# VectorE alone makes the low halves of all weight units: GpSimd's share of them is taken away

## The chip, the cores and the metric

The kernel runs on one core of a Trainium2 chip. The metric is the device time of one execution in microseconds (us), given as the median of several executions. TensorE (PE) multiplies matrices, ScalarE (ACT), VectorE (DVE) and GpSimd (POOL) do the elementwise work, and SyncE (SP) issues the weight transfers. In the profile PEld is TensorE's weight load.

## The reference

Two models of depth 2 run one after the other on 256 tokens of width 1024, in float32. What matters here is how many weights pass through:

```python
# first block, layer 0
x = layer_norm(ALPHA * x + retention_mixer(x, ret_w_in, ret_w_out))
x = layer_norm(ALPHA * x + swiglu(x, ffn_w_in, ffn_w_out))          # D_FF = 2816
# first block, layer 1
x = layer_norm(ALPHA * x + stick_breaking_mixer(x, k, v, w_q, w_out))
x = layer_norm(ALPHA * x + moe_swiglu(x, w_router, w_in, w_out))     # 8 experts, top 2, D_EXPERT = 3584
# second block, two layers
x = x + rms_norm(hybrid_mixer(rms_norm(x), w_in, ..., w_out))        # dilated attention and mLSTM
x = x + rms_norm(conv_ffn(rms_norm(x), w_up, ..., w_down))
```

Every product is a float32 one, and every weight is used once for all tokens that need it.

## The kernel before, in words

**Weight units.** All big weights are cut into 519 units of 128 partitions by 2048 columns (`UNIT`), 1 MB each, in the order of use. `Stream` (line 33) loads them ahead of use on SyncE's queue. A float32 product is made of three products of float32r parts: a unit is split into a high half `wh`, which ScalarE makes by a copy that rounds (`split_h`, line 75), and a low half `wl`, which is the unit minus its high half (`split_l`, line 89). TensorE then multiplies high by high, high by low and low by high. At most four units (three in the experts' phase) are split and not yet used up; `done()` after a unit's last product frees its place, and the next `advance()` splits the next unit.

**Who makes the low half.** `split_l` cuts the 2048 columns at `cut`: VectorE subtracts columns 0 to `cut`, GpSimd the rest, each in an instruction of its own. `W.cut` is set by hand from phase to phase, and `W.order`, if it isn't empty, gives the cuts of the next units one by one. With `cut` = UNIT VectorE makes the whole half, with 0 GpSimd does. In the first three phases (retention, ffn, stick-breaking) most units have `cut` = UNIT; in the experts' phase, the two conv_ffn phases and all their output projections it is 1408, in most of the two hybrid phases 1024.

**Joints.** Between two phases stands a joint: the last four units of the output projection are used by token tile (`tail`, line 252), so that the norm of the first 128 tokens (`joint.stats(0)`, then `joint.trans(0)`, which transposes its result and splits it) lies beside the products of the second 128. In the `advance()` calls between them the first four units of the next phase are split; their cuts are `Joint.order` = 0, UNIT, 0, 1024 (in stick-breaking 1024, 0, 0; after the experts 0, 0; at the experts' start UNIT, 0, then UNIT four times). `head` (line 273) then multiplies the first three units by the first token tile, runs `joint.trans(1)`, and multiplies the fourth.

**Order.** The program's order is the order of each engine's queue (there is no scheduler): a weight split stands in VectorE's queue where `advance()` was called, between the instructions of the norms, the gates and the attention. In the experts' phase a step is one slice of one expert: four units of its input weights and two of its output weights, 72 matmuls of 512 columns. Every second expert has a step in which `regather` (line 705) splits the 256 tokens again (line 648, two instructions on VectorE). In the last expert GpSimd also scales and adds the residual (lines 899 and 900). GpSimd's queue also issues the small transfers: gains, tables, convolution weights.

Of the kernel before, what the change touches and what calls it, by code (L numbers as in the profile page):

```python
# [10 lines left out]
F32 = mybir.dt.float32  # L11
# [5 lines left out]
OP = mybir.AluOpType  # L17
# [12 lines left out]
UNIT = 2048  # L30


class Stream:
    """Weights in units of [128, UNIT]: loaded, then split into two float32r parts, ahead of use."""

    def __init__(self, nc, pool, pairs, raws, units):
        self.nc, self.pool, self.units = nc, pool, units
        self.pairs = self.room = pairs
        self.free = [(pool, "raw%d" % i, len(units)) for i in range(raws)]
        self.order, self.cut = [], UNIT  # L40
        self.n_load = self.n_h = self.n_l = self.n_get = self.n_done = 0
        self.rt, self.ht = {}, {}

    def widen(self, slots):
        """More slots (pool, tag, end) for loads, each for units before its end."""
        self.free = slots + self.free

    def slot(self):
# [31 lines left out]
    def split_l(self):  # L80
        i = self.n_l
        if i >= self.n_h:
            return False
        (r, s), h = self.rt.pop(i), self.ht[i]
        l = self.part("wl")
        cut = self.order.pop(0) if self.order else self.cut
        for eng, s0, s1 in ((self.nc.vector, 0, cut), (self.nc.gpsimd, cut, UNIT)):
            if s0 < s1:
                eng.tensor_tensor(l[:, s0:s1], r[:, s0:s1], h[:, s0:s1].bitcast(F32), op=OP.subtract)  # L89
        self.ht[i] = (h, l)  # L90
        self.free.append(s)
        self.n_l += 1
        self.load()
        return True
# [34 lines left out]
class Net:  # L129
# [108 lines left out]
                                          start=(first and kk == 0 and i == 0), stop=(last and kk == 1 and i == 2))  # L238

    def proj_out(self, yh, yl, n, joint):  # L240
        """n units of the output projection, its last four by token tile, with the joint's parts between."""
        accs = [self.psA(), self.psA()]
        m = 4
        for u in range(n - m):
            w = self.W.get()
            for t in range(2):
                self.out_unit(accs[t], w, yh, yl, u, t, u == 0, False)
            self.W.done()
            self.W.advance()
        self.tail(accs, [(yh, yl, u) for u in range(n - m, n)], n == m, joint)  # L250

    def tail(self, accs, items, first, joint, hooks=()):
        m = len(items)
        ws = [self.W.get() for _ in range(m)]
        for i, (yh, yl, u) in enumerate(items):
            if i < len(hooks):
                hooks[i]()
            self.out_unit(accs[0], ws[i], yh, yl, u, 0, first and i == 0, i == m - 1)
        self.W.advance()
        joint.stats(0, accs[0])  # L260
        accs[1] = accs[1] or self.psA()
        for i, (yh, yl, u) in enumerate(items):
            self.out_unit(accs[1], ws[i], yh, yl, u, 1, first and i == 0, i == m - 1)
            self.W.done()
            if i == m - 2:
                joint.trans(0)
            if i in joint.early:
                self.W.advance()
        joint.stats(1, accs[1])
        if joint.order[-1] is not None:  # L270
            self.W.advance()

    def head(self, joint, table, n=4):
        """The first n units of the next projection by token tile, the second tile's joint between."""
        ws, ps = [], []
        for i in range(n):
            if i == n - 1:
                joint.trans(1)
                self.nc.scalar.preload_act_table_set(table + "_and_others")
            ws.append(self.get8())  # L280
            ps.append(self.psP([128, 2, 256]))
            self.tokB(ps[i], ws[i], 0)
        self.W.cut = UNIT
        for i in range(n):
            self.tokB(ps[i], ws[i], 1)
            self.W.done()
            yield ps[i]

    def features(self, first, n, pool):
        """The n feature-major products of a projection whose first units came by token tile."""  # L290
        nc, last = self.nc, None

        def copied(ps):
            x = pool.tile([128, 2, 256], F32, tag="fl", name="fl", bufs=2)
            nc.scalar.activation(x, ps, AF.Copy)
            return x

        def flip(x):
            pt = self.psP([128, 2, S])
            for c in range(2):  # L300
                for t in range(2):
                    nc.tensor.transpose(pt[:, c, tok(t)], x[:, t, tok(c)], self.ident)
            return pt

        k = 0
        for ps in first:
            x = copied(ps)
            if last is not None:
                yield flip(last)
            last = x  # L310
            k += 1
        ps = self.projA()
        yield flip(last)
        yield ps
        for _ in range(n - k - 1):
            yield self.projA()
# [145 lines left out]
    def stick(self, joint0):  # L462
# [107 lines left out]
        parts(7)  # L570
        joint = LayerNorm(self, o, w, 2, "kT")
        joint.early = (0, 1, 2)
        joint.order = [1024, 0, 0, None]

        def last():
            pv(6)
# [6 lines left out]
        return joint  # L583

    def open_moe(self):
        """Room for the experts' first weights, before the phase itself."""
        W = self.W
        self.mp = p = self.span.enter_context(self.tc.tile_pool(name="m1", bufs=1))
        self.moe_i = i = W.n_get
        end = i + 6 * E * SL  # L590
        W.widen([(p, "yy", i + 44)] + [(p, "more%d" % j, end) for j in range(2)])
        while W.load():
            pass

    def moe(self, joint0):
        nc, tc, a, W = self.nc, self.tc, self.a, self.W
        with self.span:
# [1 line left out]
            end = self.moe_i + 6 * E * SL  # L599
            W.widen([(self.xt, "x%d" % (self.x_tag ^ 1), self.moe_i + 46)])  # L600
            W.load()
            W.cut, W.order = 1408, [UNIT, 0] + [UNIT] * 4
            low, ones, slot = self.low[:, 0, :], self.low[:, 1, :], self.slot
            x = self.x
            X3 = {}
# [179 lines left out]
                return yh, yl  # L785

            def sums(n):
                """Both halves of an expert's output, in one or two tiles."""
                A = [self.psA() for _ in range(n)]
                if n == 1:  # L790
                    return [A[0][:, f, :] for f in range(2)], [(A[0].rearrange("p f c -> p (f c)"), slice(0, D))]
                return [x[:, 0, :] for x in A], [(A[f][:, 0, :], half(f)) for f in range(2)]
# [15 lines left out]
                        nc.vector.tensor_tensor(o, q, o, op=OP.add)  # L808

            def overflow():  # L810
                """Every expert's tokens beyond its first 128 (not run when there are none)."""
                most = nc.values_load(mci[0:1, 0:1], min_val=0, max_val=2 * S)
                ov_w, ov_x = (x.rearrange("p k s -> p (k s)") for x in self.new_xT())
                ov_h, ov_l = ov_w[:, :D], ov_w[:, D:]
# [112 lines left out]
                W.split_l()  # L927
            joint.trans(0)
            W.advance()
            W.cut = 1408  # L930
            combine(*part, 1, False)
            joint.stats(1, acc[:, 1, :])
            W.advance()
# [2 lines left out]
    def hybrid(self, l, joint0):  # L936
        nc, tc, a, W = self.nc, self.tc, self.a, self.W
        with tc.tile_pool(name="h1", bufs=1) as p, tc.tile_pool(name="h2", bufs=2) as w:
# [67 lines left out]
            dn = {}  # L1006

            def rotated(ps):
                """Queries or keys of four heads, token-major."""
                x = w.tile([128, 2, 4, 2, 32], F32, tag="cv", name="ro")  # L1010
                t1, t2 = (w.tile([128, 2, 8, 32], F32, tag="wk", name=n) for n in ("t1", "t2"))
                for t, i in ((t1, 0), (t2, 1)):
# [15 lines left out]
                    nc.scalar.activation(dst[0], ps, AF.Copy, scale=scale)  # L1028

            def attend(n):  # L1030
                """The turn of head n - 1's probabilities and the scores of head n."""
                A = self.psA()
                if n > 0:
                    x = at[:, (n - 1) % 2]
# [136 lines left out]
                nc.vector.reciprocal(rs, rs)  # L1171

            def gated(i, ps):
                """Output gates of heads 2i, 2i+1, doubled, by the gain."""
                c = slice(256 * i, 256 * i + 256)
                nc.scalar.activation(sg[:, :, c], ps, AF.Tanh, scale=0.5)
                nc.vector.scalar_tensor_tensor(sg[:, :, c], sg[:, :, c], 1.0,
                                               hg[:, None, c].to_broadcast([128, 2, 256]), op0=OP.add, op1=OP.mult)
# [5 lines left out]
                        nc.vector.scalar_tensor_tensor(y, y, rs[:, 2 * h + t:2 * h + t + 1], sg[:, t, tok(h)],  # L1184
                                                       op0=OP.mult, op1=OP.mult)

            W.cut = UNIT
            first = self.head(joint0, "natural_log_exp")
            aq = {}
            todo = {1: [(prepare,)], 3: [(gating,)], 5: [(gates, 0)], 6: [(gates, 1)], 7: [(mscores, 0), (mscores, 1)],  # L1190
# [2 lines left out]
            for u in range(14):  # L1193
# [3 lines left out]
                    i = u - 1  # L1197
                    flip([qk[:, i % 2, i // 2 * 2:i // 2 * 2 + 2]], aq.pop(i), 0, 1.0 if i % 2 else 0.125)
                c = None
                if u == 0:  # L1200
                    W.cut = 1408
                if u < 4:
                    aq[u] = rotated(ps)
                elif A:
# [25 lines left out]
                    f[0](*f[1:])  # L1230
                if u == 4:
                    nc.scalar.preload_act_table_set("exp_and_others")
                    W.cut = 1024
                if u not in (3, 13):
                    W.advance()
            mnorm()
# [11 lines left out]
    def conv_ffn(self, l, joint0):  # L1248
        nc, tc, a, W = self.nc, self.tc, self.a, self.W
        with tc.tile_pool(name="c1", bufs=1) as p, tc.tile_pool(name="c2", bufs=2) as w:  # L1250
# [4 lines left out]
            for j, ps in enumerate(self.features(self.head(joint0, "gelu_apprx_tanh"), FT, w)):  # L1255
# [4 lines left out]
                for c in range(2):  # L1260
# [2 lines left out]
                                                   op0=OP.mult, op1=OP.add)  # L1263
                    nc.vector.scalar_tensor_tensor(u[:, c, :S - 1], ps[:, c, 1:], k[:, 2:3], u[:, c, :S - 1],
                                                   op0=OP.mult, op1=OP.add)
                W.cut = 1408
                more = W.split_h()
                nc.scalar.activation(u[:, 0, :], u[:, 0, :], AF.Gelu_apprx_tanh)
                nc.vector.tensor_tensor(u[:, 0, :], u[:, 0, :], u[:, 1, :], op=OP.mult)
# [1 line left out]
                    W.split_l()  # L1271
                self.split(yh[:, j, :], yl[:, j, :], u[:, 0, :])
                W.advance()
            W.cut = 1408
            self.proj_out(yh, yl, FT // 2, joint)
            return joint


class Joint:
    early = (0, 2)  # L1280
    order = (0, UNIT, 0, 1024)

    def __init__(self, net, p, w):
        self.n, self.nc, self.p, self.w = net, net.nc, p, w
# [7 lines left out]
    def begin(self):  # L1292
        n = self.n
        self.xo = n.x
        self.xn = n.new_x()
        n.W.cut, n.W.order = 1024, [x for x in self.order if x is not None]
        self.nc.scalar.preload_act_table_set("sqrt_and_others")
        self.src = {}

# [61 lines left out]


class MoeNorm(LayerNorm, PreNorm):
    order = (0, 0)

    def __init__(self, net, p, w, i, pre):
        Joint.__init__(self, net, p, w)
        g = p.tile([128, 2, D], F32, tag="oh", name="jg")
# [196 lines left out]
```

## Time and profile before

| what | value |
|---|---|
| time, median of 3 | 2355.78 us (2352.26 to 2356.99) |
| span of the profiled execution | 2346.5 us |
| median less that span | 9.3 us |
| matmuls in the span | 13077 |
| TensorE's mean granted clock | 0.983 of full speed |
| weights and other bytes moved | 562.16 MB, 240 GB/s over the span |

The profiled execution's time outside its span is not listed by itself; its time is taken as the span and the 9.3 us that lie between it and the median, a difference that has the spread of the three executions (4.7 us) in it. The engines run side by side, so shares of busy time don't add up. A matmul's duration in the profile overlaps the next one's, so TensorE is at its peak only where its clock is 1.00 and its next matmul waits for nothing.

### The profile page before, as it was taken

How to read it: one execution, taken by the hardware profiler on the slowest of the kernel's cores; microseconds unless marked ns; L12 is line 12 of the kernel's file. 1: busy time of each engine (PE TensorE's matmuls, PEld its weight loads, DVE VectorE, ACT ScalarE, POOL GpSimd, SP SyncE). 2: the span in 40 equal slices, each digit the busy share in tenths (PEclk: the TensorE clock that was granted, in tenths of full speed). 3: DMA queues.
4: the chain of work that ended last, by engine and by line, in shares of the span. 5: the costliest groups of instructions: out<-in, count | busy, mean ns of one | idle time of the engine just before them, and what ended most of it. 6: DMA issues, size and time to landing. Idle time of an engine off the chain costs nothing. (4 is left out here: it accounts for less than half of the span.)

```text
span 2346.5 us, 33318 instructions
## 1 busy us (share of the span) xinstructions
PE 2235.6 (95%) x13077; PEld 1932.6 (82%) x13077; DVE 1739.7 (74%) x1655; ACT 1370.8 (58%) x1376; POOL 1282.4 (55%) x523
## 2 busy tenths in 40 slices
PE   8999999997999999999999999987998999999998
PEld 8997998886887788778877788766887997887996
DVE  6556554647899898988897889977775984775982
ACT  4353543564776677767776677765555654555662
POOL 4002000213899889889997889896333234434333
PEclk9999999998999999999999999998999999999999
DMA  8454554436989799979997899966334554433552
GB/s 311 144 174 155 203 188 161 171 133 260 361 321 338 258 382 353 353 286 368 350 351 289 317 372 359 352 250 225 111 111 161 198 198 162 146 108 137 198 198 72
DMA packets 80085, 562.16 MB, mean 240 GB/s; under 512 B 9072, under 2 KB 9136, under 8 KB 13488
## 3 DMA queue, kind: packets, MB, share of 16 engines
q1 hardware_dynamic: 76464, 547.39, 63.6%
q0 software_dynamic: 3456, 12.55, 1.5%
q8 instruction: 105, 1.72, 0.3%
q14 instruction: 60, 0.49, 0.1%
HBM read 558.86 MB, written 1.05 MB: 239 GB/s over the span
## 5 line engine op out<-in xcount | busy, mean ns | idle before, releaser
L89 POOL TENSOR_TENSOR wl<-raw,wh 128x640 fp32r<-128x640 f32 (+2 forms) x436 | 1200.7, 2775 | 845.8 <-ACT wh L75 749.1
L89 DVE TENSOR_TENSOR wl<-raw,wh 128x1408 fp32r<-128x1408 f32 (+2 forms) x503 | 1108.7, 2218 | 332.7 <-ACT wh L75 274.5
L75 ACT ACTIVATE wh<-raw 128x2048 fp32r<-128x2048 f32 x518 | 990.9, 1915 | 421.7 <-PE pp L750 146.1
L201 PE MATMUL pp<-xh,wh 128*128 128x256 f32 x1360 | 387.9, 285 | 7.3 <-ACT wh L195 7.3
L201 PE MATMUL pp<-xh,wl 128*128 128x256 f32 x1360 | 387.2, 285 | 0.9 <-DVE wl L89 0.9
L201 PE MATMUL pp<-xl,wh 128*128 128x256 f32 x1360 | 384.0, 282 | 0.0
L201 PEld LDWEIGHTS pp<-xh,wh 128*128 128x128 f32 x1360 | 257.7, 189 | 8.8 <-ACT wh L195 7.8
L201 PEld LDWEIGHTS pp<-xl,wh 128*128 128x128 f32 x1360 | 259.1, 191 | 0.2 <-issue 0.2
L201 PEld LDWEIGHTS pp<-xh,wl 128*128 128x128 f32 x1360 | 256.1, 188 | 2.1 <-DVE wl L89 1.1
L201 PE MATMUL pp<-wl,xh 128*128 128x256 f32 x720 | 205.1, 285 | 7.1 <-POOL wl L89 4.7
L201 PE MATMUL pp<-wh,xh 128*128 128x256 f32 x720 | 208.0, 289 | 2.1 <-DVE mix L1139 2.1
L201 PE MATMUL pp<-wh,xl 128*128 128x256 f32 x720 | 203.5, 283 | 0.0
L750 PE MATMUL pp<-wl,xh 128*128 128x512 f32 x448 | 180.2, 402 | 11.9 <-POOL wl L89 7.8
L750 PE MATMUL pp<-wl,xgh 128*128 128x512 f32 x448 | 179.6, 401 | 9.0 <-DVE wl L89 8.2
L750 PE MATMUL pp<-wh,xgh 128*128 128x512 f32 x448 | 181.1, 404 | 5.0 <-DVEq L827 5.0
L750 PE MATMUL pp<-wh,xh 128*128 128x512 f32 x448 | 180.8, 404 | 0.0
L750 PE MATMUL pp<-wh,xl 128*128 128x512 f32 x448 | 179.1, 400 | 0.0
L750 PE MATMUL pp<-wh,xgl 128*128 128x512 f32 x448 | 178.5, 398 | 0.0
L201 PEld LDWEIGHTS pp<-wl,xh 128*128 128x128 f32 x720 | 137.6, 191 | 11.2 <-POOL wl L89 6.8
L760 PE MATMUL pa<-wh,hh 128*128 128x512 f32 x448 | 142.2, 399 | 0.7 <-ACT hh L195 0.7
L760 PE MATMUL pa<-wl,hh 128*128 128x512 f32 x448 | 141.4, 397 | 0.0
L760 PE MATMUL pa<-wh,hl 128*128 128x512 f32 x448 | 141.4, 397 | 0.0
(338 smaller groups left out, 3343.6 us busy)
## 6 DMA issues: line engine op xcount, KB each, us to landing
raw<-in_moe_w_in SPq DMA_DIRECT2D x224, 1024.0 KB, 5.1
raw<-in_moe_w_out SPq DMA_DIRECT2D x112, 1024.0 KB, 5.2
raw<-in_w_up SPq DMA_DIRECT2D x44, 1024.0 KB, 4.8
raw<-in_w_in SPq DMA_DIRECT2D x28, 1024.0 KB, 5.0
raw<-in_ret_w_in SPq DMA_DIRECT2D x23, 1024.0 KB, 5.0
raw<-in_ffn_w_in SPq DMA_DIRECT2D x22, 1024.0 KB, 4.9
raw<-in_w_down SPq DMA_DIRECT2D x22, 1024.0 KB, 4.8
raw<-in_ffn_w_out SPq DMA_DIRECT2D x11, 1024.0 KB, 4.8
```

The costliest lines, as they stand in the source:

```text
L75: self.nc.scalar.activation(h, self.rt[i][0], AF.Copy)
L89: eng.tensor_tensor(l[:, s0:s1], r[:, s0:s1], h[:, s0:s1].bitcast(F32), op=OP.subtract)
L201: self.nc.tensor.matmul(out, lhsT=w, rhs=x, start=(i == 0), stop=(i == n - 1))
L750: nc.tensor.matmul(q, lhsT=x[:, k, :], rhs=ww[:, kk, :], start=(k == 0 and i == 0), stop=(k == KC - 1 and i == 2))
L760: nc.tensor.matmul(A[0][f], lhsT=x[:, k, :], rhs=ww[:, kk, half(f)], start=(s == 0 and k == 0 and i == 0), stop=(s == SL - 1 and k == 3 an ...
```

## The change

Every low half is now one VectorE instruction over all 2048 columns (the first unit, which `start` splits in quarters, was VectorE's before and stays so). `cut` and `order` are gone, with all the lines that set them; `joint.order[-1] is not None`, which also told whether the tail ends with an `advance()`, becomes `joint.after`, with the same values. The order of loads, of high halves and of all other work in the queues is as before, and comments in the code were taken out.

```diff
@@ class Stream, split_l
         (r, s), h = self.rt.pop(i), self.ht[i]
         l = self.part("wl")
-        cut = self.order.pop(0) if self.order else self.cut
-        for eng, s0, s1 in ((self.nc.vector, 0, cut), (self.nc.gpsimd, cut, UNIT)):
-            if s0 < s1:
-                eng.tensor_tensor(l[:, s0:s1], r[:, s0:s1], h[:, s0:s1].bitcast(F32), op=OP.subtract)
+        self.nc.vector.tensor_tensor(l, r, h.bitcast(F32), op=OP.subtract)
         self.ht[i] = (h, l)
...
@@ tail
-        if joint.order[-1] is not None:
+        if joint.after:
             self.W.advance()
@@ stick
-        joint.order = [1024, 0, 0, None]
+        joint.after = False
@@ moe
-            W.cut, W.order = 1408, [UNIT, 0] + [UNIT] * 4
@@ hybrid (other places that set W.cut likewise)
-                    W.cut = 1024
@@ class Joint
     early = (0, 2)
-    order = (0, UNIT, 0, 1024)
+    after = True
@@ Joint.begin
-        n.W.cut, n.W.order = 1024, [x for x in self.order if x is not None]
@@ class MoeNorm
-    order = (0, 0)
-
```

## Rows read from the trace of the kernel before

**Rows 1.** The page: busy time of each engine, share of the span, instructions.
```profile
PE 2235.6 (95%) x13077; PEld 1932.6 (82%) x13077; DVE 1739.7 (74%) x1655; ACT 1370.8 (58%) x1376; POOL 1282.4 (55%) x523
```

**Rows 2.** TensorE's waits by releaser: us in total, times, longest.
```profile
PE pp L750 <- DVE wl L89: 12.3, 3, 4.3
PE pp L750 <- POOL wl L89: 8.5, 5, 4.3
```

**Rows 3.** Stretches of the experts' phase: busy us of the engines, granted clock, DMA.
```profile
600.00:1560.00 960.00, 937.45 (x4153) 754.90 (x4152) 836.12 (x469) 669.75 (x459) 874.55 (x316) 0.99 0.89 334
780.00:800.00 20.00, 15.73 (x72) 12.67 (x71) 15.40 (x10) 10.16 (x9) 13.93 (x6) 0.91 0.79 278
1040.00:1060.00 20.00, 15.90 (x69) 12.84 (x68) 14.57 (x9) 9.60 (x8) 13.10 (x6) 0.83 0.78 281
1300.00:1320.00 20.00, 16.04 (x70) 12.83 (x69) 16.03 (x11) 10.55 (x8) 13.17 (x6) 0.91 0.81 291
```

**Rows 4.** Groups by shape, whole span: count, busy us, mean ns, idle before.
```profile
L89 DVE TENSOR_TENSOR wl<-raw,wh 128x1408 fp32r<-128x1408 f32 x395 | 877.6, 2239 | 186.4 <-ACT wh L75 128.5 <-POOL wl L89 46.3 <-PE pp L750 5.6
L89 DVE TENSOR_TENSOR wl<-raw,wh 128x2048 fp32r<-128x2048 f32 x82 | 190.2, 2323 | 113.0 <-ACT wh L75 112.9
L89 DVE TENSOR_TENSOR wl<-raw,wh 128x1024 fp32r<-128x1024 f32 x26 | 40.9, 1571 | 33.3 <-ACT wh L75 33.1
L196 DVE TENSOR_TENSOR hl<-pp,hh 128x512 fp32r<-128x512 f32 x56 | 38.0, 679 | 2.1 <-ACT hh L195 2.1
...
L89 POOL TENSOR_TENSOR wl<-raw,wh 128x640 fp32r<-128x640 f32 x395 | 1044.8, 2668 | 331.7 <-ACT wh L75 235.0 <-DVE u L1262 77.5 <-DVE wl L89 6.9
L89 POOL TENSOR_TENSOR wl<-raw,wh 128x2048 fp32r<-128x2048 f32 x15 | 73.8, 4928 | 346.3 <-ACT wh L75 346.3
```

**Rows 5.** Timeline, one unit of an output projection: start, duration, instruction, idle before.
```profile
1955.75 1.63 DVE L89 TENSOR_TENSOR wl<-raw,wh 128x1408 fp32r<-128x1408 f32 x1 [4.01 <-ACT wh L75]
1955.79 3.01 POOL L89 TENSOR_TENSOR wl<-raw,wh 128x640 fp32r<-128x640 f32 x1 [2.63 <-ACT wh L75]
```

**Rows 6.** Groups by shape in one experts' step, 653.79 to 671.29 us.
```profile
L89 DVE TENSOR_TENSOR wl<-raw,wh 128x1408 fp32r<-128x1408 f32 x6 | 16.3, 2747 | 0.1
...
L89 POOL TENSOR_TENSOR wl<-raw,wh 128x640 fp32r<-128x640 f32 x7 | 20.4, 2954 | 0.0
```

**Rows 7.** Timeline at the first `regather`: VectorE, TensorE.
```profile
778.60 4.51 DVE L648 TENSOR_TENSOR x3ol<-x,x3oh 128x1024 fp32r<-128x1024 f32 x2
...
786.04 0.51 PE L750 MATMUL pp<-wl,xgh 128*128 128x512 f32 x1 [4.27 <-DVE wl L89]
```

**Rows 8.** Timeline of the last joint but one; and a line of the chain.
```profile
2140.86 2.76 DVE L89 TENSOR_TENSOR wl<-raw,wh 128x2048 fp32r<-128x2048 f32 x1 [1.01 <-ACT wh L75]
2142.70 5.38 POOL L89 TENSOR_TENSOR wl<-raw,wh 128x2048 fp32r<-128x2048 f32 x1 [1.23 <-ACT wh L75]
2145.04 3.59 DVE L1405 TENSOR_TENSOR x<-z,x 128x512 f32<-128x512 f32 x1
2153.14 1.22 DVE L89 TENSOR_TENSOR wl<-raw,wh 128x1024 fp32r<-128x1024 f32 x1 [0.19 <-ACT wh L75]
2156.67 0.39 PE L201 MATMUL pp<-wl,xh 128*128 128x256 f32 x1 [0.58 <-POOL wl L89]
...
1822.52 97.91 PE pp L201 x816
```

**Rows 9.** Timeline of a unit in the first hybrid phase.
```profile
1727.14 1.23 DVE L89 TENSOR_TENSOR wl<-raw,wh 128x1024 fp32r<-128x1024 f32 x1 [2.27 <-ACT wh L75]
1727.18 3.45 POOL L89 TENSOR_TENSOR wl<-raw,wh 128x1024 fp32r<-128x1024 f32 x1 [9.53 <-ACT wh L75]
1729.34 1.31 DVE L1054 TENSOR_SCALAR nm<-m 128x2 f32<-128x2 f32 x1
```

**Rows 10.** Timeline, TensorE in the first joint.
```profile
216.65 0.75 PE L1308 MATMUL pp<-ident,x 128*128 128x128 f32 x3 [1.96 <-DVE x L1329]
```

**Rows 11.** Timeline, TensorE at the start of the first conv_ffn.
```profile
1815.67 0.66 PE L302 MATMUL pp<-ident,fl 128*128 128x128 f32 x4 [3.30 <-ACT fl L295]
```

More of the change, by code (lines that the diff above doesn't have):

```diff
@@ L39, in __init__ @@
         self.free = [(pool, "raw%d" % i, len(units)) for i in range(raws)]
-        self.order, self.cut = [], UNIT
         self.n_load = self.n_h = self.n_l = self.n_get = self.n_done = 0
@@ L282, in head @@
             self.tokB(ps[i], ws[i], 0)
-        self.W.cut = UNIT
         for i in range(n):
@@ L929, in moe @@
             W.advance()
-            W.cut = 1408
             combine(*part, 1, False)
@@ L1185, in mfinal @@
                                                        op0=OP.mult, op1=OP.mult)
-            W.cut = UNIT
             first = self.head(joint0, "natural_log_exp")
@@ L1199, in hybrid @@
                 c = None
-                if u == 0:
-                    W.cut = 1408
                 if u < 4:
@@ L1265, in conv_ffn @@
                                                    op0=OP.mult, op1=OP.add)
-                W.cut = 1408
                 more = W.split_h()
@@ L1273, in conv_ffn @@
                 W.advance()
-            W.cut = 1408
             self.proj_out(yh, yl, FT // 2, joint)
```

## The prediction, as it was put on record

> **What bounds the kernel now.** I read the page first: TensorE is busy 95% of the span, so no more than the rest, and what a lowered clock costs, is to be had; VectorE has 74%, GpSimd 55% [rows 1]. Next come TensorE's waits. The two that name low halves in the experts' phase are 12.3 us in three waits on VectorE's part and 8.5 us in five on GpSimd's [rows 2]. The table of stretches shows what such a wait costs beside itself: in the 20 us that begin with each of the three, TensorE's granted clock averages 0.91, 0.83 and 0.91 where 1.00 is full speed (2.4 GHz), so part of each ran at the lower level of 1.2 GHz after the idle time; (0.09 + 0.17 + 0.09) x 20 us = 7.0 us [rows 3]. In the 960 us from 600 to 1560 TensorE is idle 22.5 us in all. Outside the waits the experts' phase is bound by TensorE, and no change in the splitting makes that faster.
>
> **What the subtraction costs on the two engines.** The groups by shape hold the main clue: 1408 columns take VectorE 2239 ns, 2048 columns 2323 ns [rows 4]. The short instruction is as long as the long one, because most short ones ran beside GpSimd and most long ones did not. The timeline shows how: both parts start together, VectorE's ends after 1.63 us, GpSimd's after 3.01 us [rows 5]. If GpSimd's 640 columns begin only when VectorE is through, they take 3.01 - 1.63 = 1.4 us. So the two take turns, and a unit costs the pair about 3.0 us one after the other where VectorE alone needs 2.3. The turns go the other way too: a GpSimd unit of 5.38 us from 2142.70 ends at 2148.08, and a VectorE addition begun at 2145.04 ends 0.55 us after that, having taken 3.59 us [rows 8]; in the hybrid phase an instruction over two columns takes 1.31 us and ends at 1730.65, as GpSimd's part does (1727.18 + 3.45) [rows 9].
>
> **The change part by part.**
>
> *Work moved.* VectorE gets 395 x (2.32 - 2.24) = 32 us for the units cut at 1408, 26 x (2.32 - 1.57) = 20 us for those at 1024, and 15 x 2.32 = 35 us for GpSimd's whole ones: 87 us, against holds that end in its other instructions. GpSimd loses at least 1045 + 74 of its 1282 us [rows 1, 4]. Its instructions of line 89 and their waits go; no transfer is added, and raw buffers come free no later.
>
> *Experts, `regather`.* In a plain step of 17.5 us VectorE's six parts take 2747 ns each with no idle time and GpSimd's seven 2954 ns [rows 6]: the pair is as full as TensorE and has no slack. `regather`'s two instructions (4.51 us with the turns) then delay everything, and TensorE waits 4.27 us [rows 7]; the three waits are of this kind [rows 2]. After the change a step holds 6 x 2.32 + 2 x 0.68 = 15.3 us of VectorE work [rows 4], 2.2 us less than the step. `regather` itself should fall to an estimated 2.4 us (two times 1.22, what 1024 columns take alone [rows 8]). ScalarE's copies before it still delay the next high half, so I leave an estimated 1.2 us of each wait, and count no lowered clock behind it (a choice; the lower bound holds the other case). Gain: 12.3 + 7.0 - 3 x 1.2 = 15.7 us; bounds 6 (half of the wait left and the clock still falling) and 19.3.
>
> *Experts, the last one.* Five waits of 8.5 us [rows 2] come where GpSimd's residual work stands in its queue ahead of its parts. With no part there, the wait goes; GpSimd's residual instructions stay and still take turns with VectorE. Taken: 7; bounds 3 and 10.
>
> *Joints.* The third unit moves from GpSimd into VectorE's queue ahead of the norm of the second tile. In the joint of [rows 8] VectorE's second unit ends at 2140.86 + 2.32 = 2143.2 and its third at 2145.5; the norm's scaling comes next, an estimated 1.0 us before the addition, which then starts at 2146.5 unheld and ends an estimated 1.2 us later at most (its 512 columns are half of a 1.22 us instruction), against 2148.63. I take the chain as 1.5 us earlier. The fourth unit then begins at 2151.6 and takes 2.32 instead of 1.22 us, ready at 2154.0. Before, TensorE had half of that unit's product behind it when GpSimd's half arrived at 2156.67; half a product is 12 x 97.91/816 = 1.4 us, so it stood where it would have started at 2155.2. Gain 1.2 us each, three such joints: 3.7. The two LayerNorm joints after retention and ffn also lose the wait of 1.96 us [rows 10] but pay the same 1.1 us on the fourth unit: 2.5 each, 5. Stick-breaking's, where three units now stand ahead of VectorE's norm: 1.3. The joint after the experts, where two units move ahead of its second norm: 0. Sum 10; bounds -3 (each of seven loses 0.4) and 16.
>
> *Start of conv_ffn.* The small transfers stand behind GpSimd's part of the fourth unit; they go earlier, and VectorE's first product there is no longer held. TensorE's wait is 3.30 us [rows 11]; the second conv_ffn has a shorter one. Taken 4 for both, bounds 0 and 5.
>
> *Hybrid.* Here VectorE's chain sets the pace at places. Its part goes from 1.23 to 2.32 us, 1.1 later; but the short instruction behind it, now held until 1730.65, would end at 1727.14 + 2.32 and then what stood between 1728.37 and 1729.34 (0.97) and an estimated 0.2: 1730.63 [rows 9]. So the ten units of a phase change nothing; the starts of the phases, where the turns hold the rotary products, give an estimated 1 us each, the gating at the end 0.5. Taken 3, bounds -21 (20 units of 1.09 us, were all on TensorE's path) and 6.
>
> On splitting, the measured side is that a part of 1024 columns is ready after 1.22 us and a whole unit after 2.32, and TensorE could begin on the part [rows 4, 8]. The Trainium skill (Perfetto Trace Analysis, Optimizing Scalar/DVE Operations) says that where VectorE isn't saturated but leaves bubbles on other engines, breaking instructions up may finish work sooner, and that a saturated VectorE may hand work to GpSimd, though the port they share may spoil that. The first half speaks against one long instruction; it is the second rival's mechanism, and the row of 3.01 us for two parts is why I give it little.
>
> **Sum.** 15.7 + 7 + 10 + 4 + 3 = 39.7 us off the profiled execution: 2346.5 - 39.7 = 2306.8 of span, and with the 9.3 us between span and median 2316.
>
> **The rivals.** *VectorE becomes the bound among the experts.* Combining and gathering add to the 15.3 us of some steps and bring them to TensorE's 17.5; then the waits move rather than go, and the experts give only their lower bounds, 6 + 3: 2330. For it: VectorE is already busy 836 of 960 us [rows 3]. Against: much of that is time held. *VectorE's queue, the slower outcome.* A unit of 2.32 us in one piece stands in front of the short chains: 20 hybrid units at 1.09 and 15 moved whole units at 2.32 are 21 + 35 = 56 us; less the experts' 22.7 and conv_ffn's 4, the kernel is 29 us slower: 2385. It decides where the held time that goes is under half of the added time; in [rows 9] it is all of it. *The turns aren't what stretches the parts*, and the change does only half of what it says: TensorE's phase is full anyway, the joints win and lose, and the time stays within 0.2% (2351 to 2360). *More than forecast:* with fewer waits the clock stays at its upper level in the joints and hybrids too, and the upper bounds hold (19.3 + 10 + 16 + 5 + 6 = 56): 2299.
>
> **How the numbers follow.** Forecast near 2316 (2306 to 2326): 0.52. VectorE bound among the experts (2326 to 2345): 0.20. More than forecast (2290 to 2306): 0.17. No change: 0.05. Slower: 0.06. The range 2295 to 2342 leaves out the last two and the outer ends of the second and third. A difference under 0.2%, 4.7 us, which is also the spread of the three executions, can't be told from none: faster 0.90, same 0.04, slower 0.06.
>
> **What would show it.** In the changed kernel's groups all 395 + 82 + 26 + 15 = 518 low halves of line 89 on VectorE in one shape at 2.25 to 2.35 us, none on GpSimd; TensorE's waits on low halves under 6 us in the experts' phase and clock 1.00 after `regather`; line 648 near 1.2 us each; the addition of [rows 8] under 1 us. I am wrong if whole units take over 2.6 us beside the transfers, if the hybrid phases grow by more than 5 us each, or if the three waits are still over 3 us.

## The result, and the profile after

The changed kernel takes 2300.39 us (median of 4 executions, 2299.26 to 2307.82) against 2356.03 us (2352.26 to 2356.99), a ratio of 0.9774 with a 95% interval of 0.9756 to 0.9792: 55.6 us faster. The forecast was 2316 (2295 to 2342). The profiled execution took 2301.24 us with a span of 2299.5 us, 47.0 less than the span of before; the forecast for the span was 39.7 less.

The page's line of busy times, which answers to [rows 1]: GpSimd goes from 55% to 4%, and VectorE, which now does the work of both, from 1739.7 to 1711.3 us.

```profile
PE 2220.5 (97%) x13077; PEld 1929.2 (84%) x13077; DVE 1711.3 (74%) x1670; ACT 1373.2 (60%) x1376; POOL 88.1 (4%) x87
```

The groups by shape of the changed kernel, whole span, as [rows 4]: all 518 low halves have one shape and 2300 ns each.

```profile
L85 DVE TENSOR_TENSOR wl<-raw,wh 128x2048 fp32r<-128x2048 f32 x518 | 1187.8, 2300 | 312.7 <-ACT wh L74 295.1 <-PE pp L744 7.5 <-DVEq L821 2.3
```

VectorE's low halves take 1187.8 us in place of 877.6 + 190.2 + 40.9 = 1108.7 [rows 4], 79 more, and yet it is busy 28 us less: its other instructions, the same in number, lost 107.5 us, which was time held. Its low halves of before had held time in them too, which `pieces` below measures: 395 x (2239 - 1628) ns = 241 us. The same experts' step as in [rows 6], by shape: six whole units take 13.7 us where six short parts took 16.3.

```profile
L85 DVE TENSOR_TENSOR wl<-raw,wh 128x2048 fp32r<-128x2048 f32 x6 | 13.7, 2291 | 2.0 <-ACT wh L74 2.0
```

TensorE's waits after (us in total, times, longest; the first is the low halves waited for in the joints, the second answers to [rows 2]), and the stretch from 600 to 1560 us with the 20 us around each `regather` (columns as in [rows 3]): the waits fell from 20.8 to 2.0 us, and the clock stays at 2.4 GHz, 1.00, where it averaged 0.91, 0.83 and 0.91.

```profile
PE pp L197 <- DVE wl L85: 8.9, 6, 1.6
...
PE pp L744 <- DVE wl L85: 2.0, 3, 0.9
```

```profile
600.00:1560.00 960.00, 954.31 (x4266) 773.01 (x4265) 838.36 (x481) 688.60 (x472) 23.70 (x11) 1.00 0.91 345
770.00:790.00 20.00, 19.48 (x94) 15.83 (x93) 17.36 (x11) 15.38 (x13) 0.00 (x0) 1.00 0.89 324
1020.00:1040.00 20.00, 19.49 (x94) 15.80 (x93) 18.67 (x12) 15.36 (x12) 0.00 (x0) 1.00 0.83 303
1280.00:1300.00 20.00, 19.06 (x93) 15.48 (x92) 18.21 (x12) 14.55 (x11) 2.31 (x1) 1.00 0.88 335
```

The timeline at the first `regather` (start, duration, instruction, idle before): its two instructions take 2.36 us, forecast 2.4, where they took 4.51, and TensorE waits 0.53 us where it waited 4.27 [rows 7].

```profile
772.62 2.36 DVE L642 TENSOR_TENSOR x3ol<-x,x3oh 128x1024 fp32r<-128x1024 f32 x2
...
777.23 0.50 PE L744 MATMUL pp<-wl,xgh 128*128 128x512 f32 x1 [0.53 <-DVE wl L85]
```

The last joint but one, as [rows 8]: the addition of line 1389 (1405 before) takes 0.69 us, not 3.59, the second and third unit end before the scaling of the second norm starts, and the fourth, whole now, is ready 2.29 us after 2107.04. TensorE stands 1.65 us before it.

```profile
2096.39 4.49 DVE L85 TENSOR_TENSOR wl<-raw,wh 128x2048 fp32r<-128x2048 f32 x2 [0.55 <-ACT wh L74]
...
2101.84 0.69 DVE L1389 TENSOR_TENSOR x<-z,x 128x512 f32<-128x512 f32 x1
...
2107.04 2.29 DVE L85 TENSOR_TENSOR wl<-raw,wh 128x2048 fp32r<-128x2048 f32 x1 [0.19 <-ACT wh L74]
...
2109.38 0.39 PE L197 MATMUL pp<-wl,xh 128*128 128x256 f32 x1 [1.65 <-DVE wl L85]
```

In the hybrid phase the short instruction of [rows 9] takes 0.17 us instead of 1.31 and ends 3.19 us after its unit starts; before it was 3.51.

```profile
1690.17 2.29 DVE L85 TENSOR_TENSOR wl<-raw,wh 128x2048 fp32r<-128x2048 f32 x1 [2.27 <-ACT wh L74]
...
1693.19 0.17 DVE L1047 TENSOR_SCALAR nm<-m 128x2 f32<-128x2 f32 x1
```

**Where the span changed.** ScalarE loads an activation table where a joint begins and where the next phase's first products end; these loads stand at the same places of the program in both traces and cut the span into stages. Lengths in us, with the kernel that came out best below (`joint4`) beside them:

| stage | before | after | joint4 |
|---|---|---|---|
| up to the first joint | 195.4 | 195.6 | 195.7 |
| joint after retention | 37.1 | 33.7 | 33.6 |
| ffn | 160.2 | 164.0 | 160.2 |
| joint after ffn | 36.7 | 33.7 | 33.6 |
| stick-breaking | 99.3 | 101.8 | 99.3 |
| its joint, routing | 35.3 | 34.3 | 34.3 |
| experts | 1047.9 | 1012.2 | 1012.6 |
| joint after the experts | 27.0 | 26.6 | 26.6 |
| first hybrid | 117.6 | 118.4 | 118.5 |
| its last products | 8.9 | 7.8 | 7.8 |
| its joint | 30.2 | 28.6 | 28.6 |
| first conv_ffn | 165.0 | 163.8 | 161.3 |
| its joint | 35.0 | 33.5 | 33.5 |
| second hybrid | 118.9 | 117.1 | 116.1 |
| its last products | 8.9 | 7.8 | 7.8 |
| its joint | 30.2 | 28.6 | 28.6 |
| second conv_ffn, most of it | 163.2 | 162.2 | 161.2 |

The experts gave 35.7 of the 47.0 us. The two LayerNorm joints gave 3.4 and 3.0, and the phases behind them took 3.8 and 2.5 back. Each column is one profile. Over the seven kept profiles whose units outside the experts have the changed form, most of the joints agree to 0.1 us, ffn takes 162.8 to 164.0 and stick-breaking 100.3 to 103.3 us, but the first hybrid takes 116.3 to 118.4, the second 117.1 to 119.7, the first conv_ffn 162.2 to 165.0 and the second 162.2 to 163.8: differences of 1 to 3 us in these four are not resolved here.

Inside the experts' phase TensorE's transposes of `y`, one group in each step, are a clean mark. The step of the first `regather`, in the kernel before and after:

```profile
766.97 0.60 PE L775 MATMUL pp<-ident,y 128*128 128x128 f32 x4
790.26 0.60 PE L775 MATMUL pp<-ident,y 128*128 128x128 f32 x4
```

```profile
761.90 0.60 PE L769 MATMUL pp<-ident,y 128*128 128x128 f32 x4
779.89 0.60 PE L769 MATMUL pp<-ident,y 128*128 128x128 f32 x4
```

The step went from 23.29 to 17.99 us. So measured, the three `regather` steps gave 5.3 + 5.8 + 4.6 = 15.7 us, the steps of the last expert 11.2, the other steps in which an expert's output is combined 4.1, all the rest 2.1; most plain steps are the same to 0.01 us (17.18 in both). Marks on a VectorE instruction mislead here: by the starts of line 766 (760 after) this same kind of plain step seemed to shrink from 17.5 to 16.9 us, because that instruction itself moves about in its queue.

### The profile page after: what moved, and what is told of

The parts are those of the page before. It is cut to its first block, busy times and chain, and to the rows that moved or that the text cites. A ratio compares the mean times of both kernels' runs of the same rounds, so it can differ in the third digit from the quotient of the medians.

```text
span 2299.5 us, 31879 instructions
## 1 busy us (share of the span) xinstructions
PE 2220.5 (97%) x13077; PEld 1929.2 (84%) x13077; DVE 1711.3 (74%) x1670; ACT 1373.2 (60%) x1376; POOL 88.1 (4%) x87
## 5 line engine op out<-in xcount | busy, mean ns | idle before, releaser
L85 DVE TENSOR_TENSOR wl<-raw,wh 128x2048 fp32r<-128x2048 f32 x518 | 1187.8, 2300 | 312.7 <-ACT wh L74 295.1
L197 PEld LDWEIGHTS pp<-wh,xh 128*128 128x128 f32 x720 | 140.1, 195 | 5.8 <-issue 4.2
```

Source lines behind the costliest of these rows:

```text
L85: self.nc.vector.tensor_tensor(l, r, h.bitcast(F32), op=OP.subtract)
L197: self.nc.tensor.matmul(out, lhsT=w, rhs=x, start=(i == 0), stop=(i == n - 1))
```

## The experiments

All times are medians; each kernel is set against runs of the kernel before on the same chip (2356.09, 2352.86 and 2353.70 us in the three groups of runs).

**The changed kernel again.** No edit.

> The changed kernel again, so that the other kernels of this call can be set against it on the same chip: 2300 us, ratio 0.975 to 0.979 to the kernel before.

2302.66 us (2298.58 to 2302.95), ratio 0.977 [0.9756, 0.9785]. The result stands.

**pieces: the same cuts, all on VectorE.**

```diff
-        for eng, s0, s1 in ((self.nc.vector, 0, cut), (self.nc.gpsimd, cut, UNIT)):
+        for eng, s0, s1 in ((self.nc.vector, 0, cut), (self.nc.vector, cut, UNIT)):
```

> The kernel before, with the second part of each low half moved from GpSimd to VectorE and the cuts left where they were: two VectorE instructions where there were two engines. Theory (the two engines took turns, and GpSimd's turn of some 1.4 us for 640 columns is dearer than VectorE's): two pieces of 1408 and 640 columns take VectorE some 2.4 us together, so nearly all of the gain comes, 2295 to 2312 us. Rival (one long instruction in place of two short ones is what helps, fewer instructions to start): little of the gain comes, 2335 us or more.

2292.97 us (2291.48 to 2296.04), ratio 0.9739 [0.9725, 0.9754]: all of the gain and 10 us more than the change itself, 2 us below the range expected. The rival is out: it isn't the number of instructions. The groups by shape of `pieces`:

```profile
L89 DVE TENSOR_TENSOR wl<-raw,wh 128x1408 fp32r<-128x1408 f32 x395 | 642.9, 1628 | 143.6 <-ACT wh L75 135.0 <-DVEq L827 2.5 <-ACT xh L702 1.7
L89 DVE TENSOR_TENSOR wl<-raw,wh 128x640 fp32r<-128x640 f32 x395 | 326.0, 825 | 0.0
```

The same 395 parts of 1408 columns that took 2239 ns beside GpSimd [rows 4] take 1628 with GpSimd silent, and the other 640 columns take VectorE 825 ns. Both parts are done in 2.45 us, where the first alone took 2.24 before.

**joint4: the unit at a joint's end in two pieces.**

```diff
+        c = UNIT // 2 if self.halves else UNIT
+        for s0 in range(0, UNIT, c):
+            q = slice(s0, s0 + c)
+            self.nc.vector.tensor_tensor(l[:, q], r[:, q], h[:, q].bitcast(F32), op=OP.subtract)
@@ tail
         if joint.after:
+            self.W.halves = True
             self.W.advance()
+            self.W.halves = False
```

> The changed kernel, with only the unit that is split at the end of a joint (after the norm of its second tile) made in two VectorE pieces of 1024 columns, seven joints at most. Theory (the whole fourth unit makes TensorE wait about 1.4 us in the joints after retention and ffn, and the clock that falls there costs more than the wait): 2 to 10 us faster than the changed kernel, and granted clock near 1.00 in 230:250 and 427:447 us. Rival (the clock falls there because of the idle time earlier in the joint, and the wait is only where it shows): within 2 us of the changed kernel and the clock still under 0.9 there.

2290.73 us (2289.03 to 2294.52), ratio 0.9729 [0.9714, 0.9743], 11.9 us under the changed kernel in the same group, a little more than expected, the intervals of the two ratios apart, and the lowest median of all kernels here (`pieces` and `halves` overlap with it). The first joint shows why. In the changed kernel (timeline; then the stretch behind the joint, columns as in [rows 3]):

```profile
228.53 2.28 DVE L85 TENSOR_TENSOR wl<-raw,wh 128x2048 fp32r<-128x2048 f32 x1
...
230.87 0.58 PE L197 MATMUL pp<-wl,xh 128*128 128x256 f32 x1 [1.42 <-DVE wl L85]
231.24 0.42 PE L197 MATMUL pp<-wh,xl 128*128 128x256 f32 x1
231.46 0.41 PE L197 MATMUL pp<-wh,xh 128*128 128x256 f32 x1
...
230.00:250.00 20.00, 19.14 (x140) 19.14 (x141) 7.01 (x7) 7.50 (x9) 0.38 (x1) 0.83 0.29 113
```

In `joint4`, the same two views:

```profile
228.62 2.35 DVE L89 TENSOR_TENSOR wl<-raw,wh 128x1024 fp32r<-128x1024 f32 x2
...
229.89 0.39 PE L201 MATMUL pp<-wl,xh 128*128 128x256 f32 x1 [0.36 <-DVE wl L89]
230.12 0.28 PE L201 MATMUL pp<-wh,xl 128*128 128x256 f32 x1
230.24 0.28 PE L201 MATMUL pp<-wh,xh 128*128 128x256 f32 x1
...
230.00:250.00 20.00, 20.00 (x171) 20.00 (x172) 9.01 (x10) 10.56 (x14) 0.47 (x1) 1.00 0.56 184
```

The wait is 1.06 us longer in the changed kernel, but what costs is behind it: the matmuls then start every 0.21 to 0.22 us where they start every 0.12 in `joint4`, so they run at 1.2 GHz. The stretch loses (1.00 - 0.83) x 20 = 3.4 us; the ffn stage lost 3.8. With the first half ready 1.1 us sooner the clock stays at 2.4 GHz, and the table of stages shows the 3.8, 2.5 and 2.5 us back in ffn, stick-breaking and the first conv_ffn. For the first two other profiles agree: with that unit in two parts, on one engine or two, ffn takes 160.2 to 161.8 and stick-breaking 99.3 to 99.4 us in six kernels, under all seven with a whole unit. The rival, that idle time earlier in the joint brings the clock down, is out: the waits before this one, 0.65 and 0.79 us, are the same in both.

The Trainium skill (Perfetto Trace Analysis, Optimizing Scalar/DVE Operations) says that breaking up an instruction of an engine that isn't saturated but causes bubbles elsewhere may finish work sooner. The trace agrees at this one unit.

**halves: all units outside the experts in two pieces.**

```diff
+        c = UNIT if self.whole else UNIT // 2
@@ moe (set back where the last joint of the block begins)
+            W.whole = True
```

> The changed kernel, with every unit outside the experts' phase made in two VectorE pieces of 1024 columns, not only the unit at the end of a joint as in joint4. Theory (only that unit is waited for; the others are ready in time): 2288 to 2295 us, as joint4. Rival (pieces help wherever TensorE waits on a low half): 2285 us or less.

2293.22 us (2290.81 to 2296.12), ratio 0.9742 [0.9727, 0.9756], as `joint4`: the piece at the joint's end helps, and those at all other units outside the experts add nothing that shows. Both this and `pieces` have the piece at the joint's end in them, which accounts for `pieces` beating the change.

**dummy256 and dummy512: GpSimd works for nobody.**

```diff
         self.nc.vector.tensor_tensor(l, r, h.bitcast(F32), op=OP.subtract)
+        if self.lo + 6 <= i < self.hi:
+            d = self.junk[:, :256]
+            self.nc.gpsimd.tensor_tensor(d, h[:, :256].bitcast(F32), d, op=OP.subtract)
```

> The changed kernel, with one more GpSimd instruction for each unit of the experts' phase: it subtracts 256 columns, reading the high half and a scratch tile and writing the scratch tile, and nobody waits for it. Theory (the hold on VectorE is what cost time): GpSimd's 256 columns hold VectorE some 0.6 us a unit, so a unit costs the pair about 2.9 us again, and half or more of the experts' gain of some 37 us goes: 2318 to 2345 us. Rival (only that TensorE had to wait for GpSimd's later part cost time): no change, 2297 to 2304 us.

> As dummy256 with 512 columns in place of 256. Theory (turns): GpSimd's part alone takes an estimated 1.2 us (256 took 0.74), so a unit costs the pair 2.3 + 1.2 = 3.5 us where TensorE needs 2.87; 0.6 us for each of some 330 units is 200 us, less what falls into VectorE's gaps: 2420 to 2500 us, with VectorE's low halves of the experts at 3 us or more. Rival (GpSimd's turns fall into VectorE's gaps mostly): under 2340 us.

256 columns: 2312.64 us (2311.51 to 2315.23), ratio 0.9821 [0.9805, 0.9837], 10 us over the changed kernel. That excludes the rival, but the size was under the expected 18 to 45: the pair has 2.3 + 0.6 = 2.9 us a unit, about as much as TensorE's 17.18 / 6 = 2.86, and the turns fall into VectorE's gaps but for 5.5 us in the steps of `regather`, 3.6 in the last expert and 1.8 in the step in which the program tests whether an expert has more than 128 tokens (line 827 of the kernel before). 512 columns: 2441.99 us (2437.37 to 2450.87), ratio 1.0367 [1.0346, 1.0387], 140 us over the changed kernel, and slower than the kernel before, by work that nothing waits for. Timeline of `dummy256`:

```profile
640.01 2.29 DVE L86 TENSOR_TENSOR wl<-raw,wh 128x2048 fp32r<-128x2048 f32 x1 [0.70 <-ACT wh L75]
640.12 2.78 POOL L90 TENSOR_TENSOR junk<-wh,junk 128x256 f32<-128x256 f32 x1 [0.21 <-ACT wh L75]
643.35 0.75 POOL L90 TENSOR_TENSOR junk<-wh,junk 128x256 f32<-128x256 f32 x1 [0.44 <-ACT wh L75]
```

GpSimd's instruction takes 0.75 us by itself; begun 0.11 us after VectorE's it ends 0.60 us after it. The groups of `dummy512`, and what TensorE waited for:

```profile
L86 DVE TENSOR_TENSOR wl<-raw,wh 128x2048 fp32r<-128x2048 f32 x518 | 1423.6, 2775 | 218.6 <-ACT wh L75 203.9 <-POOL junk L90 9.1 <-PE pa L761 2.3
L90 POOL TENSOR_TENSOR junk<-wh,junk 128x512 f32<-128x512 f32 x330 | 918.5, 2783 | 215.6 <-ACT wh L75 208.1
```

```profile
PE pp L751 <- DVE wl L86: 47.4, 105, 4.7
```

The 188 units without a dummy hold 188 x 2.30 = 432 us, so the 330 with one take (1423.6 - 432) / 330 = 3.0 us: 0.7 us longer each. TensorE waits for VectorE 105 times.

**dummy_write: GpSimd writes and reads one column.**

```diff
+            self.nc.gpsimd.tensor_copy(d[:, :1], h[:, :1].bitcast(F32))
+            self.nc.gpsimd.memset(d, 0.0)
```

> The changed kernel, with a GpSimd write that reads nothing (a memset of 512 columns, behind a copy of one column that makes it start with the unit) for each unit of the experts' phase. Theory (VectorE is held where GpSimd reads from the same memory, not where it only writes): within 5 us of the changed kernel. Rival (any GpSimd instruction holds VectorE): 2315 us or more.

2302.21 us (2294.87 to 2308.01), ratio 0.9775 [0.9743, 0.9807], the changed kernel's time, though with a spread of 13 us. Its groups by shape and a piece of its timeline:

```profile
L86 DVE TENSOR_TENSOR wl<-raw,wh 128x2048 fp32r<-128x2048 f32 x518 | 1187.9, 2300 | 317.0 <-ACT wh L75 282.9 <-POOL junk L91 9.9 <-PE pp L752 7.5
L90 POOL COPY junk<-wh 128x1 f32<-128x1 f32 x330 | 597.2, 1810 | 199.3 <-ACT wh L75 187.7
L91 POOL MEMSET junk<- 128x512 f32 x330 | 173.8, 527 | 19.6
```

```profile
652.15 4.63 DVE L86 TENSOR_TENSOR wl<-raw,wh 128x2048 fp32r<-128x2048 f32 x2
652.33 2.15 POOL L90 COPY junk<-wh 128x1 f32<-128x1 f32 x1
654.54 0.53 POOL L91 MEMSET junk<- 128x512 f32 x1
```

GpSimd's copy of a single column takes 2.15 us: it reads, so it stands until VectorE's first unit of the two ends. The write behind it takes its 0.53 us during VectorE's second unit, and VectorE's 2300 ns don't change. So it is GpSimd's reading that takes turns with VectorE's subtraction of two operands, not its writing. The Trainium skill states this (SBUF — State Buffer, Who interferes with whom: a VectorE instruction with two SBUF inputs contends with a GpSimd instruction that reads SBUF, not with one that only writes), and both rows agree.

**moe_split, rest_split: the experts' units against all others.** Each has the one form among the experts' units and the other elsewhere; in `moe_split` the changed kernel gets its split back there, in `rest_split` the kernel before loses it there.

```diff
+        cut = 1408 if self.lo + 6 <= i < self.hi else UNIT     # moe_split, with the two engines' loop of before
...
+        if self.lo <= i < self.hi:                             # rest_split
+            cut = UNIT
```

> The changed kernel, with the experts' units (but for their first six) cut at 1408 again and their last 640 columns on GpSimd; all else as changed. Theory (the experts' phase holds nearly all of the gain, some 37 of 47 us): 2332 to 2342 us. Rival (the joints and the hybrid phases hold it, as 17 of the forecast's 40 us would have it): 2320 to 2328 us.

> The kernel before, with VectorE alone making the low halves of the experts' units; all other units cut as before. Theory (experts hold nearly all): 36 us under the kernel before, 2312 to 2322 us. Rival (the rest holds 17 of 40): 2326 to 2334 us.

moe_split: 2338.99 us (2335.39 to 2340.08), ratio 0.9937 [0.9917, 0.9957], 13.9 us faster than the kernel before. rest_split: 2320.13 us (2318.82 to 2322.07), ratio 0.9859 [0.9841, 0.9877], 32.7 us faster. Against the 53.4 us of the whole change in the first group the experts hold some 33 to 40 us (32.7 in the one, 53.4 - 13.9 = 39.5 in the other) and the joints and other phases 14 to 21; both times lie where the theory had them. In the stages it is sharper: the experts take 1012.5 us in `rest_split`, 1049.6 in `moe_split`, 1047.9 before and 1012.2 after. TensorE's waits in `moe_split` are those of [rows 2] again:

```profile
PE pp L749 <- DVE wl L89: 12.3, 3, 4.3
...
PE pp L749 <- POOL wl L89: 7.8, 4, 4.3
```

**plain_split, special_split: which steps.** The changed kernel with the cut at 1408 in some of the experts' steps; `special_split` has the condition without `not`.

```diff
+                    W.share = not (e == 7 or (e in (1, 3, 5) and s > 3))
...
+        cut = 1408 if self.share else UNIT
```

> The changed kernel, with the units of the experts' plain steps cut at 1408 again (640 columns on GpSimd), but not those split from the step of each regather to the end of its expert, nor those of the last expert. Theory (the plain steps gave some 9.5 us by waits too short to be named, and the steps of regather and the last expert the rest by themselves): 8 to 14 us over the changed kernel. Rival (in the full plain steps a backlog builds up that is paid at regather, so that the plain steps' cuts are what costs): 20 us or more over the changed kernel.

> The complement of plain_split: cut at 1408 only in the units split from the step of each regather to the end of its expert, and in the last expert. Theory: 20 to 28 us over the changed kernel. Rival (backlog from the plain steps): 15 us or less over the changed kernel. The two together should make about the 36 us of moe_split over the changed kernel if the parts simply add.

plain_split: 2315.02 us (2306.07 to 2317.03), ratio 0.9826 [0.9806, 0.9846], 12 to 15 us over the changed kernel. special_split: 2320.04 us (2319.24 to 2326.21), ratio 0.9863 [0.9843, 0.9882], 17 to 20 over: under the theory's 20 to 28 and over the rival's 15. By TensorE's marks `plain_split` loses nothing at `regather` (18.0 us a step) or in the last expert, and 5.8 us in the steps that combine and in small amounts of 0.1 to 0.4; of the rest of its loss 2.5 us lie at the experts' start, and the others outside the phase, where nothing was changed. `special_split` loses 9.9 of the 15.7 at `regather` and all 11.2 in the last expert. So the theory's parts hold, but not its reason for the plain steps (they didn't shrink), and 5.8 of the 15.7 us of `regather` need full steps ahead of it as well: the rival had a part. Neither kernel alone shows these.

**cut1792: GpSimd keeps 256 columns.** The kernel before with 1792 in place of 1408.

> The kernel before, with 1792 in place of every cut at 1408, so that GpSimd's part is 256 columns in place of 640. Theory (turns): the pair takes some 2.05 + 0.6 = 2.65 us a unit in place of 3.0, under the 2.9 us that TensorE needs, and half to three quarters of the experts' gain comes: 2318 to 2336 us. Rival (only GpSimd's lateness counts, and a short part is early): as good as the changed kernel or better, 2295 to 2308 us.

2322.86 us (2319.02 to 2325.87), ratio 0.9874 [0.9852, 0.9896]: where the theory had it, and 20 us over the changed kernel, which a short and early part should have matched. Its timeline repeats the turn: VectorE ends at 662.70, GpSimd 0.59 us later.

```profile
660.67 2.03 DVE L89 TENSOR_TENSOR wl<-raw,wh 128x1792 fp32r<-128x1792 f32 x1 [0.79 <-ACT wh L75]
660.71 2.58 POOL L89 TENSOR_TENSOR wl<-raw,wh 128x256 fp32r<-128x256 f32 x1 [0.24 <-ACT wh L75]
```

## Why the prediction was right, and where its sum was not

| term of the sum | forecast | measured in the span |
|---|---|---|
| `regather` | 15.7 | 15.7 |
| last expert | 7 (3 to 10) | 11.2 |
| other experts' steps | 0 | 6.2 |
| experts' start, up to the first transposes | 0 | 2.6 |
| joints, with what follows them | 10 (-3 to 16) | 6.3 |
| conv_ffn | 4 (0 to 5) | 2.1 |
| hybrids, with their last products | 3 (-21 to 6) | 3.2 |
| up to the first joint | 0 | -0.2 |
| sum | 39.7 | 47.1 |

**What the subtraction costs on the two engines.** Right. The turns that were read from two rows are shown by five kernels (`pieces`, `dummy256`, `dummy512`, `dummy_write`, `cut1792`): dummies that nobody waits for cost time where they read, and none where they write.

**`regather`.** Right in place and mechanism; that the size fits to the tenth is luck. The waits kept 2.0 us, not 3 x 1.2, so 10.3 went; what is left for the clock that no longer falls is 5.4, not 7.0. The two errors of 1.6 cancel. The estimate of two instructions at 2.4 us came out at 2.36.

**The last expert.** Right in mechanism, under-sized. I counted five waits of 8.5 us as its own and no clock. One of the five, 0.73 us, stands at the experts' start; four, 7.8 us, are the last expert's, as in `moe_split` above. In the kernel before the 20 us that hold its longest wait show 0.91, which is 1.8 us more:

```profile
584.64 0.50 PE L750 MATMUL pp<-wl,xgh 128*128 128x512 f32 x1 [0.73 <-POOL wl L89]
...
1560.00:1580.00 20.00, 15.70 (x62) 11.75 (x61) 14.75 (x8) 9.97 (x7) 19.54 (x9) 0.91 0.65 229
```

7.8 + 1.8 = 9.6 of the 11.2. The same correction stood in the term for `regather` and was left out here.

**"Outside the waits the experts' phase is bound by TensorE."** Right for the plain steps (17.18 and 17.18 us). What failed is the reading that the two rows of waits are all there is: the steps that combine an expert's output gave 4.1 us. In the waits of before two other rows hold 3.0 of them: TensorE for `yy`, a product that stands in VectorE's queue among the low halves (2.3 us, of which 0.6 is in the last expert), and the one wait behind that test of line 827, put down to VectorE's queue, which goes from 5.0 to 3.7 us:

```profile
PE pa L799 <- DVE yy L783: 2.3, 4, 0.6
PE pp L750 <- DVEq L827: 5.0, 1, 5.0
```

```profile
PE pp L744 <- DVEq L821: 3.7, 1, 3.7
```

The row of `yy` is gone after. What gave the other 3.2 of the 6.2 us, and the 2.6 at the experts' start beyond its wait of 0.73, is not shown. A held engine is late with all its work, and I looked for the releaser `wl` alone.

**Joints.** Over-sized by 3.7 us. The two LayerNorm joints were to give 2.5 us each, net; they gave 3.4 and 3.0, and the phases behind took 3.8 and 2.5: -0.4 and 0.5 instead of 5. The step that failed is "pay the same 1.1 us on the fourth unit": the 1.1 us is there, but the clock that falls behind it was not in the price, and `joint4` shows that this unit's form alone decides it. The three joints with RMS norm were to give 1.2 each and gave 1.6, 1.5 and 1.6; the fourth unit's longer wait (1.65 us, 0.58 before) stands behind them, in the next stage. Stick-breaking's gave 1.0 (1.3), the one after the experts 0.4 (0).

**conv_ffn.** Right in mechanism, over-sized. The wait of 3.30 us fell to 0.4:

```profile
1775.67 0.66 PE L297 MATMUL pp<-ident,fl 128*128 128x128 f32 x4 [0.37 <-ACT fl L290]
```

The stage gained only 1.2 of these 2.9 us. The rest was lost again at the joint's fourth unit: in `joint4` the first conv_ffn stage is 2.5 us shorter still.

**Hybrid.** The unit of 2.29 us in one piece cost nothing that shows: the phases changed by +0.8 and -1.8 us, within what the profiles scatter. The gating at the end, taken at 0.5 us, gave 1.1 in each of the two: four of its instructions took 3.27 us beside GpSimd and take 1.13 now.

```profile
1761.82 3.27 DVE L1184 SCALAR_TENSOR_TENSOR mix<-mix,rs,sg 128x128 f32<-128x128 f32 x4
...
1726.67 1.13 DVE L1177 SCALAR_TENSOR_TENSOR mix<-mix,rs,sg 128x128 f32<-128x128 f32 x4
```

The 1 us taken for the start of each phase is not resolved.

**Time around the span.** The 9.3 us was no time around the span. Of the changed kernel's executions each shows both, and 1.7 to 1.8 us lie between. The 25 executions of the kernel before in the later groups have spans of 2347.2 to 2358.2 us at mean clocks of 0.983 to 0.979; the profiled one, 2346.5 at 0.983, was shorter than any. So the table above accounts for the 47.0 us between the two profiles; the medians lie 55.6 apart, and where the kernel before loses the other 8.6 in most of its executions no kept trace shows, only that most of them have the lower clocks. Of the miss of 14.9 us against the profiled execution (2316.1 by the sum, 2301.24 measured) 7.3 are the sum's and 7.6 (9.3 - 1.7) this.

**The rivals.** VectorE as the experts' bound: excluded, with 838 of 960 us busy and TensorE waiting 2.0 us for it; `dummy512` shows what that case would look like. VectorE's queue, the slower outcome: excluded in the hybrids, but its mechanism is real at one place, the fourth unit of a joint, for the 11.9 us that `joint4` won. No change: excluded. "More than forecast" named 2299, within 2 us of the result, by another way: it took the upper bounds of the joints, the conv_ffn and the hybrids, none of which was reached; the time came from the experts, and 8.6 of the 55.6 us don't stand between the two profiles at all. That it fits is luck.

## What to carry to other kernels

Before an elementwise job is shared between VectorE and GpSimd, compare the duration of VectorE's part beside GpSimd with the same part alone: where a part with two operands is as long as the whole (2239 against 2323 ns here), suspect that the engines take turns, and try it without GpSimd's share, or with one that only writes. When a stall is costed, look at the granted clock of the stretch behind it too: 1.1 us of waiting at a joint cost 2.5 to 3.8 us in three phases, and cutting that one instruction in two brought them back. Cut in pieces where somebody waits; elsewhere it gained nothing here. And measure a step by marks on the engine that bounds it.

## What the runs showed of the hardware that was not expected

A GpSimd copy of one column beside VectorE's two-operand subtraction takes 1810 ns on average and 177 at the least, so most of it is standing, while a write of 512 columns takes 527 ns and disturbs nothing. GpSimd work that nobody waits for slowed this kernel by 140 us (`dummy512`), and no wait of TensorE in its trace names GpSimd: 47.4 us of them are put down to VectorE's low halves.
